# Splitting expert weights one ahead, and a position table in two rounds of products

## The chip, the cores and the metric

The kernel runs on one core of a Trainium2 chip. The metric is the device time of one execution in microseconds (us). The core has five engines that run at the same time and wait for each other through semaphores: TensorE (PE) multiplies, VectorE (DVE) and ScalarE (ACT) do elementwise work and empty PSUM, GpSimd (POOL) here mostly issues indirect transfers, and SyncE (SP) issues most other transfers. Each engine works through its own instructions strictly in order.

## The reference

A decoder layer on 1024 tokens of width 1024: attention and a convolution (they end before the part that is changed), then a mixture of experts, then a last norm. What matters here:

```python
grp = argmax(g_logits)                      # one of 4 groups, then 2 of its 8 experts per token
eid = grp * 8 + top_idx                     # 32 experts, 2048 assignments
buf_tok, buf_w = tokens and weights of each expert, sorted by expert
def expert_block(xblk, e):
    return (silu(xblk @ w_gate[e]) * (xblk @ w_up[e])) @ w_down[e]     # 1024 -> 512 -> 1024, float32
out[tok] += y * w                           # sum of the two experts of each token
```

Each expert has three weights of 2 MB, all 32 experts are read, and which tokens go to which expert is known only after routing.

## The kernel before, in words

The mixture runs over 32 *positions* e = 0 to 31. Positions 0 to 3 serve experts 0 to 3 with up to 128 tokens each. Positions 4 to 31 serve the other experts in an order that the kernel works out on the chip from the token counts: the 13 positions in `PK` take experts with at most 64 tokens ("packed"), position `XP` = 17 takes the fullest one and a second helping of 64 tokens (index `E`), the rest have 128.

**Weights.** The 96 weights are read in the order of the list `uses`: (e,0) gate, (e,1) up, (e-1,2) down, and so on. `load_to` issues them on SP's queue into a ring of eight slots of 2 MB, each as two halves of 1 MB (line 595), so a load waits until the weight eight places before it has left its slot. For positions from 4 on the load needs the expert's number, which SP reads from the tile `pos` (line 925).

**Unpacked positions** multiply in a split form: ACT rounds a quarter of a weight (128x1024) to `ehi` (line 102), DVE computes the rest `elo` (line 105), and PE makes three products of 128x512 for each of two k (lines 1024 to 1026 for gate and up, 1099 to 1101 for down). There are `NP` = 4 pairs of buffers, that is, one whole weight. `products` takes a quarter, multiplies, and calls `split_next`, which splits the next quarter in the list `pieces`. That list holds only the 57 unpacked weights. Once a weight's quarters are split, its slot is free.

**Packed positions** use the weight as it was loaded (lines 1014 and 1082), with two halves of the array side by side. So between two unpacked weights in `pieces` there can be up to three packed ones in `uses`: after (5,1) come (4,2), (6,0), (6,1), all packed, and then (5,2). Before the change the quarters of (5,2) are split while (5,1) is multiplied.

**Order.** PE, DVE and ACT run in the order in which the loop at the end of the function is written (a manual schedule). Each piece of a gate or up weight is followed by one `tick`, which takes one step from the list `todo`: a position's turn of its hidden rows, the scaling of its output, or a step of `position_tables`.

**Position table.** `position_tables` is a generator. It counts tokens per expert, ranks the experts, writes `pos`, and reorders the tokens' table `tb` into `half_t` and `late_t`, which the gathers from position 4 on need. Eight of its steps are queued in e = 0, the rest in e = 1. Nine of its steps have products on PE (lines 1138, 1143, 1168 and 1169, 1178 twice, 1187 and 1189 four times), each into the same PSUM tile `py`, and each is read by DVE before the next may write it.

Of the kernel before, what the change touches and what calls it, by code (L numbers as in the profile page):

```python
# [9 lines left out]
F32 = mybir.dt.float32  # L10
# [3 lines left out]
OP = mybir.AluOpType  # L14
# [5 lines left out]
D = 1024  # L20
H = 8
E = 32
F = 512
CW = 31
P = 128
# [8 lines left out]
LO = 4  # L34
XP = 17
# [8 lines left out]
def trunk_kernel(ctx, tc, x, c, w_mod, b_mod, g_norm1, w_in, conv_w, conv_b, conv_ln_g, conv_ln_b,  # L44
                 w_out, g_norm2, w_rg, b_rg, w_re, b_re, w_gate, w_up, w_down, g_final,
                 alibi, cst, out):
    nc = tc.nc
    x = x[0]
# [21 lines left out]
    ident = consts.tile([P, P], F32, name="ident")  # L70
    nc.sync.dma_start(ident, cst[:, 0:P])
    ones = consts.tile([P, P], F32, name="ones")
# [863 lines left out]
        split(hi, lo, wt[u][:, 2 * j:2 * j + 2, :])  # L936
        parts[u, j] = hi, lo

    def split_next():
        if pieces:  # L940
            u, j = pieces.pop(0)
            load_to(u)
            split_w(u, j)
# [10 lines left out]
    def products(u, mm, last=None):  # L954
        for j in range(4):
            if u[0] > E:
                split_w(u, j)
            mm(j, *parts.pop((u, j)))
            if j == 3 and last:
                last()  # L960
            if u[0] < E:
                split_next()
            yield

    def run(g):
# [33 lines left out]
    def gate_up(e, i):  # L999


        u = e, i
        o = st["o", e, i] = psg.tile([P, F], F32, name=("pg", "pu")[i])
        if e in PK or e == E:
            w = wt[XP if e == E else e, i]
            x4 = st["x", e]
            if e == E:
                xs = x4.rearrange("p a (b t) -> p (a b) t", b=2)
                x = lambda k: xs[:, k, :]
            else:  # L1010
                x = lambda k: x4[:, k % 4, k // 4 * 64:k // 4 * 64 + 64]
            for k in range(8):
                for c in range(2):
                    nc.tensor.matmul(o[64 * c:64 * c + 64, 0:256], x(k), w[:, k, 256 * c:256 * c + 256],  # L1014
                                     start=(k == 0), stop=(k == 7), skip_group_check=True)
                if k % 2:
                    yield
        else:
            xh, xl = st["x", e]

            def mm(j, hi, lo):
                for kk in range(2):
                    k = 2 * j + kk
                    nc.tensor.matmul(o, xh[:, k, :], hi[:, kk, :], start=(k == 0), stop=False)  # L1024
                    nc.tensor.matmul(o, xh[:, k, :], lo[:, kk, :], start=False, stop=False)  # L1025
                    nc.tensor.matmul(o, xl[:, k, :], hi[:, kk, :], start=False, stop=(k == 7))  # L1026

            yield from products(u, mm, (lambda: hidden(e)) if i else None)
        if i == 0:
            hs = st["h", e] = moe.tile([P, F], F32, name="hs")  # L1030
            n = 256 if e in PK or e == E else F
            nc.scalar.activation(hs[:, 0:n], o[:, 0:n], AF.Silu)
        elif e in PK or e == E:
            hidden(e, 256)
# [39 lines left out]
    def down(e):  # L1074

        t = st.pop(("t", e))
        if e in PK or e == E:
            wd = wt[XP if e == E else e, 2].rearrange("p (k a) f -> p k (a f)", a=2)
            py = psg.tile([P, F], F32, name="pg") if e == E else psx.tile([P, D], F32, name="py")[:, 0:512]
            for k in range(4):  # L1080
                for g in range(2):
                    nc.tensor.matmul(py[64 * g:64 * g + 64, :], t(k), wd[:, k, 512 * g:512 * g + 512],
                                     start=(k == 0), stop=(k == 3), skip_group_check=True)
                yield
            o2 = [(slice(64 * g, 64 * g + 64), slice(0, 512), py[64 * g:64 * g + 64, :],
                   slice(512 * g, 512 * g + 512)) for g in range(2)]
            if e == E:
                si, ws = [t[:, E - LO:E - LO + 1] for t in half_t]
            else:
                si, ws = slots(e)  # L1090
            w, n = 512, 2
        else:
            hh, hl = t
            py = psx.tile([P, D], F32, name="py")
            halves = [py[:, 0:512], py[:, 512:1024]]

            def mm(k, hi, lo):
                for half, o in enumerate(halves):
                    nc.tensor.matmul(o, hh[:, k, :], hi[:, half, :], start=(k == 0), stop=False)  # L1099
                    nc.tensor.matmul(o, hh[:, k, :], lo[:, half, :], start=False, stop=False)  # L1100
                    nc.tensor.matmul(o, hl[:, k, :], hi[:, half, :], start=False, stop=(k == 3))  # L1101

            yield from products((e, 2), mm)
            o2 = [(slice(0, P), slice(512 * i, 512 * i + 512), o, slice(512 * i, 512 * i + 512))
                  for i, o in enumerate(halves)]
            si, ws = slots(e)
            w, n = D, 1
        ys = moe.tile([P, D], F32, name="ys")[:, 0:w]

        def scale(i):  # L1110
            ps, sl, o, gl = o2[i]
            v.scalar_tensor_tensor(ys[ps, sl], o, ws[ps], gt2b[ps, gl], op0=OP.mult, op1=OP.mult)  # L1112
            if i:
                scatter(ys, si, n)

        todo.extend([lambda: scale(0), lambda: scale(1)])

    def pth(p, n):
        return psx.tile([P, D], F32, name="py")[0:p, 0:n]
# [12 lines left out]
    def position_tables():  # L1132
# [1 line left out]
        tmp = Scratch()  # L1134
        n = E - LO

        pb = pth(P, E)
        nc.tensor.matmul(pb, ones, Cc, start=True, stop=True)
        yield
        kb = tmp(P, E)  # L1140
        v.scalar_tensor_tensor(kb, pb, float(E), iota[:, 0:E], op0=OP.mult, op1=OP.add)
        pc = pth(E, 1)
        nc.tensor.matmul(pc, Cc, ones[:, 0:1], start=True, stop=True)
        yield
        cnt, kc, first, r = [tmp(E, 1) for i in range(4)]
        v.tensor_copy(cnt, pc)
        v.scalar_tensor_tensor(kc, cnt, float(E), tok1[0:E, 0:1], op0=OP.mult, op1=OP.add)
        v.tensor_scalar(first, tok1[0:E, 0:1], LO + 0.5, float(P), op0=OP.is_lt, op1=OP.mult)
        yield
# [1 line left out]
        v.tensor_scalar(m, kb[0:E, LO:], kc, None, op0=OP.is_lt)  # L1151
        v.tensor_reduce(r, m, axis=AX.X, op=OP.add)
        v.tensor_add(r, r, first)
        pi = tmp(E, n)
        v.tensor_scalar(pi, rankp[0:E, :], r, None, op0=OP.is_equal)
        yield

        v.tensor_mul(m, pi, capp[0:E, :])
        v.tensor_reduce(caps[:, 0:1], m, axis=AX.X, op=OP.add)
        v.tensor_add(caps[:, 0:1], caps[:, 0:1], first)  # L1160
        v.tensor_sub(cnt, cnt, caps[:, 0:1])
        v.tensor_scalar(cnt, cnt, float(P), None, op0=OP.add)
# [1 line left out]
        nb = tmp(E, 8)  # L1164
        v.tensor_tensor(nb, cnt.to_broadcast([E, 8]), lev[0:E, :], op=OP.is_gt)
        v.tensor_reduce(caps[:, 1:2], nb, axis=AX.X, op=OP.add)
        pp = pth(1, E + 1)
        nc.tensor.matmul(pp[:, LO:E], tok1[0:E, 0:1], pi, start=True, stop=True)
        nc.tensor.matmul(pp[:, E:E + 1], caps[:, 1:2], ones[0:E, 0:1], start=True, stop=True)
        yield  # L1170
        v.tensor_scalar(pos[:, LO:E], pp[:, LO:E], -1.0, None, op0=OP.add)
        v.tensor_copy(pos[:, E:E + 1], pp[:, E:E + 1])

        tT = moe.tile([P, D], F32, name="ys")[0:E, :].rearrange("e (q a s) -> e q a s", q=2, a=4)
        for q in range(2):
            pt = pth(E, 4 * P)
            for a in range(4):
                nc.tensor.matmul(pt[:, a * P:a * P + P], tb[:, a, q, :], ident, start=True, stop=True)
            yield
            v.tensor_copy(tT[:, q], pt.rearrange("e (a s) -> e a s", a=4))  # L1180

        def by_position(q, c0, c1, dst, halves=False):
            pt = pth(P, 4 * (c1 - c0))
            for a in range(4):
                sl = slice(a * (c1 - c0), (a + 1) * (c1 - c0))
                for h in range(2) if halves else ():
                    nc.tensor.matmul(pt[64 * h:64 * h + 64, sl], tT[:, q, a, 0:64], pi[:, c0:c1], start=True, stop=True)
                if not halves:
                    nc.tensor.matmul(pt[:, sl], tT[:, q, a, :], pi[:, c0:c1], start=True, stop=True)
            yield  # L1190
            t = tmp(P, 4 * (c1 - c0))
            v.tensor_copy(t, pt)
            tables(t.rearrange("p (a e) -> p a e", a=4), dst, moe, halves)

        yield from by_position(0, 0, n, [t[:, 0:n] for t in half_t], True)
        yield from by_position(0, 0, n, [t[:, 0:n] for t in late_t])
        x = XP - LO
        yield from by_position(1, x, x + 1, [t[:, n:n + 1] for t in late_t])
        yield from by_position(1, x, x + 1, [t[:, n:n + 1] for t in half_t], True)

    def overflow_tables():

# [73 lines left out]

    with tc.manual_schedule(engines={mybir.EngineType.PE, mybir.EngineType.DVE, mybir.EngineType.Activation}):
        for n in range(NP):
            split_next()
        for f in steps(0):  # L1280
            f()
        table = position_tables()
        for e in range(E):
            load_to((e, 0))
            if e < 2:
# [132 lines left out]
```

## Time and profile before

| | |
|---|---|
| median of 3 runs | 1235.61 us (1233.15 to 1236.14) |
| the profiled execution | 1232.49 us, of which the span from first to last instruction is 1230.7 us |
| busy over the span | PE 88%, DVE 64%, ACT 42%, POOL 18% |
| read from HBM, written | 275.75 MB, 26.23 MB |
| mean granted TensorE clock | 0.933 of full speed |

The mixture's first products start at 604.94 us and its last end before 1200 us; after it, the sum is read back, normed and written. Shares over the whole span mix the attention, the start of the mixture and its long even stretch, so they have to be read stretch by stretch. Times in the rows below are from the start of the span.

### The profile page before, as it was taken

Reading aid. Unit: us, or ns where it says so; the run is one execution under the profiler, and the core shown is the slowest. Engines: PE = TensorE matmul, PEld = TensorE weight load, DVE = VectorE, ACT = ScalarE, POOL = GpSimd, SP = SyncE. Lnnn points to the kernel's source line nnn. Section 1 sums busy time; section 2 is a strip of 40 time slices with the busy share of each in tenths; the row PEclk is TensorE's granted clock in tenths of the full one; section 3 lists DMA queues with packets and bytes.
Section 4 is the critical chain, followed back from the end, with each engine's and each line's share of the span. In section 5 each row is a group of like instructions: output and inputs, shape, how many; then the busy total and the mean of one; then the engine's idle time right before and its main releaser. Section 6 shows DMA issues by size and latency. Waiting matters only on the chain. (4 is left out here: it accounts for less than half of the span.)

```text
span 1230.7 us, 16064 instructions
## 1 busy us (share of the span) xinstructions
PE 1088.1 (88%) x5876; PEld 795.1 (65%) x5876; DVE 790.8 (64%) x1307; ACT 517.1 (42%) x795; POOL 223.2 (18%) x204
## 2 busy tenths in 40 slices
PE   4899999998999999999366999997979999799980
PEld 0667777786666667888344877775746677577750
DVE  1458999993664567676533976664645477566753
ACT  1431111114767653232222765553535455455622
POOL 2340000006121105001300222221211123112112
PEclk9899999998999999999666999998989999989995
DMA  9542534202001018538532999999999999999947
GB/s 366 185 154 92 216 127 147 103 12 74 20 17 36 1 59 304 214 131 306 198 122 76 309 376 406 409 407 388 390 383 353 398 392 402 380 399 392 371 117 283
DMA packets 60828, 292.65 MB, mean 238 GB/s; under 512 B 11861, under 2 KB 16213, under 8 KB 33092
## 3 DMA queue, kind: packets, MB, share of 16 engines
q1 hardware_dynamic: 48020, 253.16, 52.5%
q0 software_dynamic: 11296, 34.17, 9.8%
q10 hardware_dynamic: 1424, 4.20, 0.8%
q8 instruction: 48, 0.79, 0.3%
q14 instruction: 40, 0.33, 0.1%
HBM read 275.75 MB, written 26.23 MB: 245 GB/s over the span
## 5 line engine op out<-in xcount | busy, mean ns | idle before, releaser
L105 DVE TENSOR_TENSOR elo<-raw,ehi 128x1024 fp32r<-128x1024 f32 x228 | 273.3, 1223 | 113.9 <-ACT ehi L102 110.0
L102 ACT CAST ehi<-raw 128x1024 fp32r<-128x1024 f32 x228 | 237.9, 1049 | 159.6 <-PE pg L1026 55.5
L317 DVE SCALAR_TENSOR_TENSOR cv<-cv,cwT 128x1024 f32<-128x1024 f32 x120 | 154.1, 1284 | 3.6
L269 PE MATMUL pb<-hT,whi 128*128 128x512 f32 x256 | 100.8, 394 | 1.7 <-POOL hT L98 1.3
L268 PE MATMUL pb<-hT,whi 128*128 128x512 f32 x256 | 101.8, 399 | 0.0
L270 PE MATMUL pb<-hT,wlo 128*128 128x512 f32 x256 | 100.4, 393 | 0.6 <-DVE wlo L105 0.6
L1069 POOL DMA_INDIRECT x1d<-ys,ti x19 | 40.2, 2116 | 133.8 <-DVE ys L1112 127.0
L1024 PE MATMUL pg<-ehi,xh 128*128 128x512 f32 x152 | 64.0, 421 | 0.0
L1038 DVE TENSOR_TENSOR hs<-hs,pu 128x512 f32<-128x512 f32 (+1 forms) x33 | 18.9, 572 | 69.2 <-PE pu L1014 64.3
L1024 PE MATMUL pu<-ehi,xh 128*128 128x512 f32 x152 | 62.4, 410 | 0.0
L1099 PE MATMUL py<-ehi,hh 128*128 128x512 f32 x152 | 62.3, 410 | 0.0
L268 PEld LDWEIGHTS pb<-hT,whi 128*128 128x128 f32 x256 | 48.1, 188 | 21.8 <-ACT whi L102 9.2
L1025 PE MATMUL pu<-elo,xh 128*128 128x512 f32 x152 | 61.6, 405 | 0.0
L1026 PE MATMUL pu<-ehi,xl 128*128 128x512 f32 x152 | 61.5, 405 | 0.0
L1025 PE MATMUL pg<-elo,xh 128*128 128x512 f32 x152 | 61.4, 404 | 0.0
L1026 PE MATMUL pg<-ehi,xl 128*128 128x512 f32 x152 | 61.3, 403 | 0.0
L1100 PE MATMUL py<-elo,hh 128*128 128x512 f32 x152 | 59.6, 392 | 0.0
L1101 PE MATMUL py<-ehi,hl 128*128 128x512 f32 x152 | 59.5, 391 | 0.0
L269 PEld LDWEIGHTS pb<-hT,whi 128*128 128x128 f32 x256 | 48.1, 188 | 13.1 <-POOL hT L98 2.9
L1014 PE MATMUL pg<-raw,x 128*64 128x256 f32 x448 | 56.4, 408 | 0.0
L270 PEld LDWEIGHTS pb<-hT,wlo 128*128 128x128 f32 x256 | 48.1, 188 | 10.7 <-DVE wlo L105 1.0
L916 POOL DMA_INDIRECT xe<-h2d,ti x20 | 26.5, 1327 | 147.2 <-PE pt L994 121.2
(274 smaller groups left out, 2242.1 us busy)
## 6 DMA issues: line engine op xcount, KB each, us to landing
raw<-in_w_exp_gate_dram SPq DMA_DIRECT2D x64, 1024.0 KB, 19.5
raw<-in_w_exp_up_dram SPq DMA_DIRECT2D x64, 1024.0 KB, 23.2
raw<-in_w_exp_down_dram SPq DMA_DIRECT2D x64, 1024.0 KB, 21.3
wm<-in_w_mod_dram POOLq DMA_DIRECT2D x16, 1024.0 KB, 5.1
wm<-in_w_mod_dram SPq DMA_DIRECT2D x8, 1024.0 KB, 9.6
raw<-in_w_in_dram SPq DMA_DIRECT2D x3, 2048.0 KB, 9.7
xt<-in_x_dram SPq DMA_DIRECT2D x8, 512.0 KB
raw<-in_w_in_dram SPq DMA_DIRECT2D x4, 1024.0 KB, 11.9
```

What stands on the lines that cost most here:

```text
L102: nc.scalar.copy(hi, src)
L105: nc.vector.tensor_sub(lo, src, hi.bitcast(F32))
L268: nc.tensor.matmul(p[half], hi[:, k, :], hT[0][:, k, sl], start=(k == 0), stop=False)
L269: nc.tensor.matmul(p[half], hi[:, k, :], hT[1][:, k, sl], start=False, stop=False)
L270: nc.tensor.matmul(p[half], lo[:, k, :], hT[0][:, k, sl], start=False, stop=(k == 7))
L317: nc.vector.scalar_tensor_tensor(y, u[:, j:j + T], w, y, op0=OP.mult, op1=OP.add)
L1024: nc.tensor.matmul(o, xh[:, k, :], hi[:, kk, :], start=(k == 0), stop=False)
L1025: nc.tensor.matmul(o, xh[:, k, :], lo[:, kk, :], start=False, stop=False)
L1026: nc.tensor.matmul(o, xl[:, k, :], hi[:, kk, :], start=False, stop=(k == 7))
L1099: nc.tensor.matmul(o, hh[:, k, :], hi[:, half, :], start=(k == 0), stop=False)
L1100: nc.tensor.matmul(o, hh[:, k, :], lo[:, half, :], start=False, stop=False)
L1101: nc.tensor.matmul(o, hl[:, k, :], hi[:, half, :], start=False, stop=(k == 3))
```

## The change

It has two parts. (1) `split_next` now splits a quarter only if its weight is at most one place in `uses` after the weight being multiplied, and only if a pair of buffers is free; packed positions call it too, after every second k of gate and up and after every k of down. (2) `position_tables` has two rounds of products in place of nine. The first (counts, and the transposes of `tb`) is issued before position 0's own transposes, and ACT copies it out of PSUM. The second (the positions, and all four reorderings) is one run of products in e = 0 behind an empty step, and ACT copies it out; DVE's steps then read only SBUF. `pos` is written in the ninth step in place of the seventh.

```diff
+    at = {u: n for n, u in enumerate(uses)}
+    def split_next(now):
-        if pieces:
+        if pieces and len(parts) < NP and at[pieces[0][0]] <= now + 1:
             u, j = pieces.pop(0)
             load_to(u)
             split_w(u, j)
...
             if u[0] < E:
-                split_next()
+                split_next(at[u])
             yield
...
                 if k % 2:
+                    split_next(at[XP if e == E else e, i])
                     yield
...
+                split_next(at[XP if e == E else e, 2])
                 yield
...
-        pb = pth(P, E)
-        nc.tensor.matmul(pb, ones, Cc, start=True, stop=True)
+        pc = psx.tile([P, 4, P], F32, name="pth").rearrange("p a b -> p (a b)")
+        nc.tensor.matmul(pc[:, 0:E], ones, Cc, ...)
+        nc.tensor.matmul(pc[0:E, E:E + 1], Cc, ones[:, 0:1], ...)
+        pt = psx.tile([P, D], F32, name="py")[0:E, :]
+        for q in range(2):
+            for a in range(4):
+                nc.tensor.matmul(pt[:, (4 * q + a) * P:(4 * q + a + 1) * P], tb[:, a, q, :], ident, ...)
+        pb = tmp(P, E + 1)
+        nc.scalar.copy(pb[:, 0:E], pc[:, 0:E])
+        nc.scalar.copy(pb[0:E, E:E + 1], pc[0:E, E:E + 1])
+        tT = moe.tile([P, D], F32, name="ys")[0:E, :]
+        for q in range(2):
+            nc.scalar.copy(tT[:, 512 * q:512 * q + 512], pt[:, 512 * q:512 * q + 512])
         yield
...
+        yield
+        yield
+        pp = psx.tile([P, D], F32, name="py")
+        c = pp[:, 0:512]
+        nc.tensor.matmul(pp[0:1, 512 + LO:512 + E], tok1[0:E, 0:1], pi, ...)
+        nc.tensor.matmul(pp[0:1, 512 + E:512 + E + 1], caps[:, 1:2], ones[0:E, 0:1], ...)
+        jobs = ((0, 0, n, True), (1, x, x + 1, True), (0, 0, n, False), (1, x, x + 1, False))
+        for q, c0, c1, halves in jobs:
+            for a in range(4):
...
+        t = tmp(P, o)
+        nc.scalar.copy(t, c[:, 0:o])
+        pe = tmp(1, E + 1)
+        nc.scalar.copy(pe[:, LO:E + 1], pp[0:1, 512 + LO:512 + E + 1])
+        yield
+        yield
+        v.tensor_scalar(pos[:, LO:E], pe[:, LO:E], -1.0, None, op0=OP.add)
+        for (o, w), (q, c0, c1, halves) in zip(cols, jobs):
+            tables(t[:, o:o + 4 * w]..., d, moe, halves)
             yield
...
         for n in range(NP):
-            split_next()
+            split_next(0)
+        table = position_tables()
+        next(table)
         for f in steps(0):
             f()
-        table = position_tables()
```

## Rows read from the trace of the kernel before

**Rows 1.** Stretches of the span (start:end in us, length, busy time of each engine).

```profile
core 0: us, PE busy (x) PEld busy (x) DVE busy (x) ACT busy (x) POOL busy (x), PEclk, DMA share, GB/s
600.00:678.00 78.00, 49.68 (x186) 36.97 (x187) 27.12 (x58) 20.17 (x23) 2.03 (x3) 0.62 0.34 117
678.00:829.00 151.00, 151.00 (x838) 114.83 (x837) 114.50 (x122) 91.76 (x109) 31.87 (x19) 1.00 1.00 384
...
1076.00:1174.00 98.00, 94.46 (x492) 70.43 (x493) 71.47 (x76) 57.10 (x69) 18.17 (x10) 0.96 0.99 378
1174.00:1200.00 26.00, 21.51 (x128) 13.86 (x126) 11.56 (x14) 5.40 (x7) 4.52 (x3) 0.98 0.42 98
700.00:720.00 20.00, 20.00 (x95) 16.73 (x95) 19.51 (x20) 16.20 (x18) 6.95 (x3) 1.00 1.00 358
```

**Rows 2.** Timeline of SP's queue: weight loads (start us, us, instruction, count).

```profile
598.08 2.60 SPq L595 DMA_DIRECT2D raw<-in_w_exp_gate_dram  x2
...
650.65 13.23 SPq L595 DMA_DIRECT2D raw<-in_w_exp_gate_dram  x2
677.34 4.42 SPq L595 DMA_DIRECT2D raw<-in_w_exp_up_dram  x2
...
1161.20 2.81 SPq L595 DMA_DIRECT2D raw<-in_w_exp_down_dram  x2
```

**Rows 3.** Timeline of PE, positions 0 and 1 (brackets: idle before, releaser).

```profile
604.94 0.77 PE L1024 MATMUL pg<-ehi,xh 128*128 128x512 f32 x1
...
607.64 0.47 PE L1138 MATMUL py<-Cc,ones 128*128 128x32 f32 x2
...
629.98 1.91 PE L1178 MATMUL py<-ident,tb 128*32 128x128 f32 x8 [2.54 <-DVE pos L1172]
...
639.64 1.12 PE L994 MATMUL pt<-ident,xe 128*128 128x128 f32 x4
...
643.79 0.77 PE L1024 MATMUL pg<-ehi,xh 128*128 128x512 f32 x1
...
656.44 1.87 PE L1189 MATMUL py<-ys 32*128 32x28 f32 x8 [2.67 <-DVE ys L1192]
...
671.09 1.02 PE L1187 MATMUL py<-ys 32*64 32x1 f32 x16 [2.56 <-DVE ys L1192]
...
678.56 0.60 PE L994 MATMUL pt<-ident,xe 128*128 128x128 f32 x4
...
685.35 0.48 PE L1024 MATMUL pg<-ehi,xh 128*128 128x512 f32 x1
...
690.91 0.39 PE L1024 MATMUL pu<-ehi,xh 128*128 128x512 f32 x1
```

**Rows 4.** Timeline of ACT, one split in the same stretch.

```profile
653.81 1.04 ACT L102 CAST ehi<-raw 128x1024 fp32r<-128x1024 f32 x1 [4.75 <-PE pg L1026]
```

**Rows 5.** Timeline of DVE: the table's input, and what stands ahead of one round.

```profile
594.98 0.42 DVE L883 COPY tb<-ptab 128x256 f32<-128x256 f32 x1
...
654.89 1.23 DVE L105 TENSOR_TENSOR elo<-raw,ehi 128x1024 fp32r<-128x1024 f32 x1 [3.68 <-ACT ehi L102]
656.03 0.27 DVE L1192 COPY ys<-py 128x112 f32<-128x112 f32 x1
```

**Rows 6.** Waits from 600 to 1200 us (total us, times, longest).

```profile
ACT ehi L102 <- DMA raw<-in_w_exp_down_dram: 37.4, 10, 11.0
```

**Rows 7.** Timeline of ACT, the last long stall.

```profile
1074.47 1.99 ACT L102 CAST ehi<-raw 128x1024 fp32r<-128x1024 f32 x2 [2.01 <-DMA raw<-in_w_exp_down_dram]
```

**Rows 8.** Timeline of PE around it.

```profile
1065.78 3.65 PE L1082 MATMUL py<-raw,h 128*64 128x512 f32 x16
...
1077.43 1.13 PE L1063 MATMUL pth<-ident,hs 128*128 128x128 f32 x4 [8.00 <-DVE hs L1038]
...
1084.27 3.62 PE L1014 MATMUL pu<-raw,x 128*64 128x256 f32 x32
...
1088.29 0.49 PE L1099 MATMUL py<-ehi,hh 128*128 128x512 f32 x1
```

More of the change, by code (lines that the diff above doesn't have):

```diff
@@ L937, in split_w @@
         parts[u, j] = hi, lo
-    def split_next():
-        if pieces:
+    at = {u: n for n, u in enumerate(uses)}
+    def split_next(now):
+        if pieces and len(parts) < NP and at[pieces[0][0]] <= now + 1:
             u, j = pieces.pop(0)
@@ L1135, in position_tables @@
         n = E - LO
-        pb = pth(P, E)
-        nc.tensor.matmul(pb, ones, Cc, start=True, stop=True)
+        pc = psx.tile([P, 4, P], F32, name="pth").rearrange("p a b -> p (a b)")
+        nc.tensor.matmul(pc[:, 0:E], ones, Cc, start=True, stop=True, skip_group_check=True)
+        nc.tensor.matmul(pc[0:E, E:E + 1], Cc, ones[:, 0:1], start=True, stop=True, skip_group_check=True)
+        pt = psx.tile([P, D], F32, name="py")[0:E, :]
+        for q in range(2):
+            for a in range(4):
+                nc.tensor.matmul(pt[:, (4 * q + a) * P:(4 * q + a + 1) * P], tb[:, a, q, :], ident, start=True, stop=True,
+                                 skip_group_check=True)
+        pb = tmp(P, E + 1)
[4 more added lines that the diff above has]
+            nc.scalar.copy(tT[:, 512 * q:512 * q + 512], pt[:, 512 * q:512 * q + 512])
+        tT = tT.rearrange("e (q a s) -> e q a s", q=2, a=4)
         yield
         kb = tmp(P, E)
[L1141 to L1146, printed above, removed]
+        v.scalar_tensor_tensor(kb, pb[:, 0:E], float(E), iota[:, 0:E], op0=OP.mult, op1=OP.add)
+        cnt = pb[0:E, E:E + 1]
+        kc, first, r = [tmp(E, 1) for i in range(3)]
         v.scalar_tensor_tensor(kc, cnt, float(E), tok1[0:E, 0:1], op0=OP.mult, op1=OP.add)
@@ L1153, in position_tables @@
         v.tensor_add(r, r, first)
+        yield
         pi = tmp(E, n)
         v.tensor_scalar(pi, rankp[0:E, :], r, None, op0=OP.is_equal)
-        yield
         v.tensor_mul(m, pi, capp[0:E, :])
         v.tensor_reduce(caps[:, 0:1], m, axis=AX.X, op=OP.add)
+        yield
         v.tensor_add(caps[:, 0:1], caps[:, 0:1], first)
@@ L1166, in position_tables @@
         v.tensor_reduce(caps[:, 1:2], nb, axis=AX.X, op=OP.add)
-        pp = pth(1, E + 1)
-        nc.tensor.matmul(pp[:, LO:E], tok1[0:E, 0:1], pi, start=True, stop=True)
-        nc.tensor.matmul(pp[:, E:E + 1], caps[:, 1:2], ones[0:E, 0:1], start=True, stop=True)
         yield
-        v.tensor_scalar(pos[:, LO:E], pp[:, LO:E], -1.0, None, op0=OP.add)
-        v.tensor_copy(pos[:, E:E + 1], pp[:, E:E + 1])
-        tT = moe.tile([P, D], F32, name="ys")[0:E, :].rearrange("e (q a s) -> e q a s", q=2, a=4)
@@ L1175, in position_tables @@
-        for q in range(2):
-            pt = pth(E, 4 * P)
-            for a in range(4):
-                nc.tensor.matmul(pt[:, a * P:a * P + P], tb[:, a, q, :], ident, start=True, stop=True)
-            yield
[L1180 to L1199, printed above, removed]
+        yield
+        pp = psx.tile([P, D], F32, name="py")
+        c = pp[:, 0:512]
+        nc.tensor.matmul(pp[0:1, 512 + LO:512 + E], tok1[0:E, 0:1], pi, start=True, stop=True, skip_group_check=True)
@@ new lines, in position_tables @@
+        nc.tensor.matmul(pp[0:1, 512 + E:512 + E + 1], caps[:, 1:2], ones[0:E, 0:1], start=True, stop=True,
+                         skip_group_check=True)
+        x = XP - LO
+        jobs = ((0, 0, n, True), (1, x, x + 1, True), (0, 0, n, False), (1, x, x + 1, False))
+        o = 0
+        cols = []
+        for q, c0, c1, halves in jobs:
+            w = c1 - c0
+            for a in range(4):
+                sl = slice(o + a * w, o + a * w + w)
+                for h in range(2) if halves else ():
+                    nc.tensor.matmul(c[64 * h:64 * h + 64, sl], tT[:, q, a, 0:64], pi[:, c0:c1], start=True, stop=True,
+                                     skip_group_check=True)
+                if not halves:
+                    nc.tensor.matmul(c[:, sl], tT[:, q, a, :], pi[:, c0:c1], start=True, stop=True, skip_group_check=True)
+            cols.append((o, w))
+            o += 4 * w
@@ new lines, in position_tables @@
+        t = tmp(P, o)
[3 more added lines that the diff above has]
+        yield
+        yield
+        v.tensor_scalar(pos[:, LO:E], pe[:, LO:E], -1.0, None, op0=OP.add)
+        v.tensor_copy(pos[:, E:E + 1], pe[:, E:E + 1])
+        for (o, w), (q, c0, c1, halves) in zip(cols, jobs):
+            d = [t_[:, n:n + 1] if q else t_[:, 0:n] for t_ in (half_t if halves else late_t)]
+            tables(t[:, o:o + 4 * w].rearrange("p (a e) -> p a e", a=4), d, moe, halves)
+            yield
```

## The prediction

> **What bounds the kernel now.** I read the span stretch by stretch first, because the whole-span shares mix phases. The mixture has three phases. From 600 to 678 us nothing is busy: PE 49.68 of 78 us at a granted clock of 0.62, the DMA engines 0.34, 117 GB/s. From 678 to 1174 us the DMA engines are busy all the time at 378 to 384 GB/s, while PE is busy 151 of 151 us at first and 94.46 of 98 at the end. From 1174 us the transfers fall off (0.42) and PE still works off 21.51 us [rows 1]. So the long stretch is a stream of weights with PE close behind it, and it is early or late as a whole: its start is set by the first phase, its tail by how far PE lags when the last weight lands.
>
> Why is the first phase slow? SP's queue shows the loads waiting for slots: the ninth weight (gate of position 3) is issued at 598.08, the twelfth (gate of position 4) only at 650.65, the thirteenth at 677.34 [rows 2]. A slot opens when its weight has been split, and a quarter is split when PE has used up the one before. So the stream waits for PE. PE in turn shows a repeating pattern: from the round of table products at 656.44 to the one at 671.09 are two rounds, 7.3 us each, with six matmuls of real work between rounds and an idle of 2.56 to 2.67 us before each that DVE ends [rows 3]. The chain is serial: six matmuls end, ACT splits (1.04 us), DVE splits (1.23), DVE reads the table's last product (0.27), and only then may PE issue the next table product, with the matmuls of the expert queued behind it [rows 3 to 5]. The six matmuls, which need none of this, wait in line. That PE runs at the low one of its two clocks there (0.62 on average, against 1.00 from 678 us on) is a consequence of these gaps [rows 1].
>
> From four products of experts' weights, (0,0), (0,1), (1,0), (1,1), the first phase makes 604.94 to 678.56 = 73.6 us [rows 3].
>
> **The table, rebuilt step by step.** With the rounds gone, the same stretch costs:
> - Four weights at the pace of an undisturbed one, 685.35 to 690.91 = 5.56 us: 22.2 us [rows 3].
> - The clock is low at the start. Before, the first six matmuls took 604.94 to 607.64 = 2.70 us, where a quarter at the pace above is 1.39. I take two quarters at that price, +2.6; bounds: one quarter (+1.3), all sixteen (+21) if the clock never rises. The last is not likely, since PE then has no gaps [rows 3].
> - Transposes of position 1 and the turn of position 0, 639.64 to 643.79: 4.2 us, unchanged (3 if the clock is high) [rows 3].
> - Second round of products: two sets like 656.44 (1.87) and two like 671.09 (1.02), 5.8 us at the low clock, half at the high one, and at worst one wait as before (2.67). I take 5; bounds 3 and 8.4 [rows 3].
> - DVE's small steps. Each is at most as long as the copy at 656.03 (0.27), some four to five per step, so up to 1.1 us; with a split (1.23) they pass the 1.39 us that a quarter takes PE, in about four steps of position 1. Overrun up to 4.4, I take 2; none if they fit [rows 3, 5].
>
> Sum 22.2 + 2.6 + 4.2 + 5 + 2 = 36.0 against 73.6: the stretch ends **37.6 us** earlier (bounds 31.8, from 22.2 + 2.6 + 4.2 + 8.4 + 4.4 = 41.8, and 44, from 22.2 + 1.3 + 3 + 3 = 29.5).
>
> What moves is covered. The first round can start when `tb` is copied (594.98 + 0.42 = 595.4); its eight transposes are two groups like 629.98, 1.91 each [rows 3, 5]. The counts add less than 1, so it ends near 600.2 and leaves the time until the products at 604.94, in which PE has only position 0's transposes. If that cover were gone it would cost 4.8 us once. The four copies that ACT takes over are single instructions; priced like a quarter's split (1.04) they are 4.2 us and end near 604 at worst, so they may hold the first x split by a microsecond. `pos` moves two steps later. On SP only the twelfth load and what is queued behind it wait for it; the slot for that load opens when (1,1) has been split, later than the ninth step, so the move costs nothing. It would cost only if `pos` came after that.
>
> **Does the stream follow?** In the new first phase four loads have to be issued in some 40 us in place of 79: that is 2 MB in about 10 us, well under 384 GB/s [rows 1, 2]. From the thirteenth load on, the slots open at the same pace as before, so I shift the whole stream by the 37.6 us. A small debt is possible: before, the twelfth weight had landed when the thirteenth was issued, now it is still on its way (2 MB at 384 GB/s, 5.4 us); as in 700 to 720 us the stream runs at 358 GB/s for want of free slots, it can catch up there [rows 1]. I count 0, bound -4.
>
> **The split bound.** ACT waited ten times, 37.4 us in all, for a down weight still in flight [rows 6]. That is a weight up to four places ahead in `uses`: nine of the 57 unpacked weights have three packed ones before them. The wait stands in ACT's and DVE's queues ahead of work that is due. At 1074.47 ACT begins the second pair of splits of such a weight, whose half has just landed, and the hidden rows (line 1038) of the present position are queued behind them on DVE; PE idles 8.00 us at 1077.43, although the two packed weights it should multiply next were loaded earlier [rows 7, 8]. With the bound the split comes behind them. PE is free at 1065.78 + 3.65 = 1069.4; turn 1.13, gate and up 3.62 each, transposes 0.60 (as at 678.56): 1078.4 instead of 1088.29 for the first product of the late weight, whose second half landed by 1074.47, so it is not late [rows 3, 7, 8]. Gain 9.9 us of PE's lag.
>
> For the earlier stalls of this kind I count nothing: the DMA engines are saturated through them, and PE meets the stream again. The last one counts, because the stretch behind it (94.46 of 98 us busy) has no slack in which the lag was made up, and PE still has 21.51 us of work when the transfers fall off [rows 1]. I take **9** for it; bounds 0 (the stream holds PE back instead) and 10. Calling `split_next` in packed positions adds no instruction, it moves 16 weights' splits into the packed weight just before. That weight takes PE 3.62 us; four splits of 1.23 on DVE take 4.9, behind one of 1.04 on ACT, but PE needs one quarter per 1.39 us, so only the first is waited for, if any [rows 3 to 5, 8].
>
> Sum 37.6 + 9 = 46.6 from the profiled 1232.49: 1185.9. The median of the runs is 3.1 above the profiled execution, so I forecast 1189.
>
> **Rivals.**
> - *Only the table pays.* The stalls on weights in flight reappear as PE's own waits for the same weights and the tail stays: 1235.6 - 37.6 = 1198. For it: the DMA engines are never idle after 678 us, so PE can't win over the whole stretch [rows 1].
> - *More than forecast.* Clock up at once, no overrun, 10 in the tail: 1235.6 - 54 = 1182 and, if slots also open sooner where PE lagged, some 4 less, 1178.
> - *The stream can't keep its rate.* If it ran at 358 GB/s, as in 700 to 720 us, throughout, the 496 us from 678 to 1174 would be 532, +36, and 1225 would result. Against it: that row is short of slots, and the three long rows show 378 to 384 [rows 1]. The Trainium skill (DMA: Bandwidth & Descriptors, Where 436 GB/s comes from) has the HBM side bind at about 358 GB/s for loads into SBUF; by that rule the stream's length would come out as in this rival. The trace's 384 over 151 us is above it, so I give it little.
> - *Late splits (slower).* Sixteen unpacked weights come straight after a packed one. If their splits start only when PE stands at the weight, each costs 1.04 + 1.23 = 2.3 us, 36 us in all [rows 4, 5]; from 2.9 us each, with no stream to hide it, the gain of 46.6 is eaten, and at 4 us the time is 1253. For it: a packed weight is shorter than four splits. Against it: ACT and DVE have little else to do there.
> - *No change.* The first phase is bound by something else, the gathers or the loads of the first eight weights. Against it: the idle of PE there is ended by DVE each time [rows 3].
>
> **How the numbers follow.** Forecast 1189 (its own range 1181 to 1195): 0.58. Only the table: 0.18. More: 0.12. Rate lost or a first phase that stays slow, 1204 to 1225: 0.07. No change 0.02, late splits to the point of a loss 0.03. The low end takes in the "more" case with a microsecond of margin, 1177; the high end takes the table alone at its bound, 1235.6 - 31.8 = 1204. Range 1177 to 1204 leaves out the last three cases and some edges, under 2 in 10. About 0.3%, 3.7 us, is what a measurement can tell from no change. Faster 0.95, same 0.02, slower 0.03.
>
> **What would show it.** In the changed profile: no idle of PE on DVE between quarters of position 0, one at most before the second round; (1,1) ends near 641; the thirteenth load is issued near 640 and the DMA share is 1.00 from about 650; ACT's waits for down weights fall from 37.4 us to a few, and PE's 8 us stalls on line 1038 go; the last load is issued near 1124 and PE's tail after it is shorter by some 9 us. Wrong if the thirteenth load comes after 650, if the rate of the stream is under 375 GB/s, or if PE waits for splits after packed weights.

## The result, and the profile after

The changed kernel takes 1195.88 us (median of 4 runs, 1194.77 to 1199.56) against 1235.18 before (median of 4): a ratio of 0.9689, 95% interval [0.9664, 0.9714]. The forecast was 1189, range 1177 to 1204, and faster. The profiled execution went from 1232.49 to 1195.03 us, its span from 1230.7 to 1193.2, so 37.5 us are to be found in the trace.

Stretches of the changed kernel's span, in the columns of [rows 1]:

```profile
600.00:642.00 42.00, 35.04 (x167) 28.85 (x168) 23.25 (x48) 20.97 (x26) 2.42 (x3) 0.80 0.56 192
643.00:795.00 152.00, 152.00 (x839) 115.36 (x838) 115.42 (x123) 91.15 (x109) 35.13 (x20) 1.00 1.01 392
795.00:1140.00 345.00, 325.16 (x1787) 230.24 (x1785) 216.02 (x230) 170.36 (x207) 71.24 (x40) 0.99 1.00 382
1140.00:1166.00 26.00, 13.97 (x78) 7.93 (x74) 7.82 (x10) 2.48 (x5) 5.41 (x3) 0.92 0.44 97
```

The first phase ends at 642 instead of 678 us. From there the DMA engines are busy all the time again, at 382 to 392 GB/s, and the stretch is as long as before. SP's queue says the same; compare [rows 2], where the thirteenth weight went at 677.34 and the last at 1161.20:

```profile
598.46 2.60 SPq L595 DMA_DIRECT2D raw<-in_w_exp_gate_dram  x2
...
637.95 2.85 SPq L595 DMA_DIRECT2D raw<-in_w_exp_gate_dram  x2
643.48 3.21 SPq L595 DMA_DIRECT2D raw<-in_w_exp_up_dram  x2
...
1125.73 2.83 SPq L595 DMA_DIRECT2D raw<-in_w_exp_down_dram  x2
```

The thirteenth load is 33.9 us earlier, the last 35.5. Between them lie 483.9 us before and 482.3 after: the stream is shifted, not shortened.

PE in the first phase, which answers to [rows 3] (lines have moved: 1028 to 1030 are the products of 1024 to 1026, 997 the transposes of 994, 1148 the transposes of `tb`, 1202 and 1205 the reorderings):

```profile
595.84 3.40 PE L1148 MATMUL py<-ident,tb 128*32 128x128 f32 x16 [0.60 <-DVE tb L883]
601.95 0.92 PE L997 MATMUL pt<-ident,xe 128*128 128x128 f32 x4 [2.71 <-DMA xe<-h2d,ti]
...
605.09 0.78 PE L1028 MATMUL pg<-ehi,xh 128*128 128x512 f32 x1
...
616.72 0.21 PE L1189 MATMUL py<-ys,cs 32*1 32x28 f32 x2
618.20 0.18 PE L1190 MATMUL py<-ones,caps 32*1 32x1 f32 x2 [1.27 <-DVE caps L1183]
618.32 1.09 PE L1202 MATMUL py<-ys 32*64 32x28 f32 x32
619.34 3.56 PE L1205 MATMUL py<-ys 32*128 32x28 f32 x16
622.83 0.80 PE L1028 MATMUL pu<-ehi,xh 128*128 128x512 f32 x1
...
625.56 0.91 PE L997 MATMUL pt<-ident,xe 128*128 128x128 f32 x4
...
629.80 0.78 PE L1028 MATMUL pg<-ehi,xh 128*128 128x512 f32 x1
...
642.30 0.61 PE L997 MATMUL pt<-ident,xe 128*128 128x128 f32 x4
```

The first round is done before the gather has landed (601.95). After it there is one wait on DVE for the table, 1.27 us, where the kernel before had nine, of 0.49 to 4.04 us and 23.9 us in all. (1,1) ends at 642.30, where it ended at 678.56 [rows 3].

The stalls on a down weight in flight have not gone, they are spread. These are waits of the changed kernel between 640 and 1165 us (total us, times, longest; ACT's for weights in flight, and PE's first three); before, ACT had 37.4, 10, 11.0 for down weights [rows 6]:

```profile
ACT ehi L102 <- DMA raw<-in_w_exp_down_dram: 36.7, 13, 6.5
...
ACT ehi L102 <- DMA raw<-in_w_exp_up_dram: 8.3, 7, 2.5
...
ACT ehi L102 <- DMA raw<-in_w_exp_gate_dram: 3.3, 6, 0.8
...
PE py L1104 <- ACT ehi L102: 6.7, 4, 2.8
PE py L1105 <- DVE elo L105: 4.4, 7, 0.8
PE pu L1017 <- DMA raw<-in_w_exp_up_dram: 4.2, 5, 1.5
```

PE no longer stands 8 us at a turn [rows 8]; it waits a few us at a time for weights that have just landed. That is the rival's picture, "PE's own waits for the same weights". All the same PE idles less: in the stretch of 345 us that answers to 795 to 1140, it was busy for 316.77 us before and for 325.16 after.

```profile
829.00:1174.00 345.00, 316.77 (x1744) 227.49 (x1743) 216.60 (x228) 172.18 (x207) 66.93 (x40) 0.96 1.00 384
```

### The profile page after: what moved, and what is told of

Read it like the earlier page. It is cut to its first block, busy times and chain, and to the rows that moved or that the text cites. A ratio compares the mean times of both kernels' runs of the same rounds, so it can differ in the third digit from the quotient of the medians.

```text
span 1193.2 us, 16040 instructions
## 1 busy us (share of the span) xinstructions
PE 1079.5 (90%) x5876; PEld 788.5 (66%) x5876; DVE 784.2 (66%) x1300; ACT 514.3 (43%) x801; POOL 232.0 (19%) x204
## 5 line engine op out<-in xcount | busy, mean ns | idle before, releaser
L102 ACT CAST ehi<-raw 128x1024 fp32r<-128x1024 f32 x228 | 234.1, 1049 | 101.5 <-DMA raw<-in_w_exp_down_dram 36.7
L1073 POOL DMA_INDIRECT x1d<-ys,ti x19 | 44.9, 2361 | 129.2 <-DVE ys L1117 114.3
L1028 PE MATMUL pu<-ehi,xh 128*128 128x512 f32 x152 | 59.9, 394 | 0.0
L1017 PE MATMUL pu<-raw,x 128*64 128x256 f32 x448 | 51.6, 381 | 4.2 <-DMA raw<-in_w_exp_up_dram 4.2
L422 ACT ACTIVATE ns<-ns,st 128x128 f32<-128x128 f32 (+7 forms) x64 | 49.2, 772 | 9.2 <-DVE st L418 8.6
```

Source lines behind the costliest of these rows:

```text
L102: nc.scalar.copy(hi, src)
```

## The experiments

Two theories. **S**: the stream of weights sets the time from the thirteenth load on; the table moved its start, and the split bound can only shorten what PE has left after the last loads, some 3 us. **R**: the split bound is worth the 9 us that were predicted, and the table's part lost as much on the way.

One table serves all runs. Each entry is the start (us) of an instruction in that run's own trace: position 0's first transposes, the transposes behind (1,1), the thirteenth and the last weight's load, PE's last group (down of position 31), the first read-back of the sum. The first column moves by 5 us from run to run with what comes before the mixture, so the text compares differences between columns. Those of the first phase have a spread of their own: in the seven runs whose first phase is the changed kernel's, x(0) to (1,1) is 40.1 to 40.4 us in four and 38.5 in three (less stream with the old split, tail order, scale first), so there a difference under 2 us tells nothing.

| run | x(0) | (1,1) done | 13th load | last load | last group | read-back |
|---|---|---|---|---|---|---|
| before | 601.65 | 678.56 | 677.34 | 1161.20 | 1192.91 | 1205.40 |
| changed | 601.95 | 642.30 | 643.48 | 1125.73 | 1153.85 | 1167.82 |
| changed again | 602.43 | 642.82 | 644.18 | 1125.58 | 1153.69 | 1167.26 |
| table only | 598.81 | 638.95 | 639.96 | 1121.84 | 1153.22 | 1165.60 |
| bound only | 603.13 | 680.09 | 678.87 | 1163.18 | 1194.35 | 1206.69 |
| round twice | 598.93 | 644.01 | 645.40 | 1126.54 | 1154.67 | 1168.54 |
| less stream | 604.22 | 644.34 | 645.35 | 1099.65 | 1129.22 | 1141.55 |
| less stream, old split | 603.28 | 641.81 | 643.23 | 1094.34 | 1130.65 | 1143.73 |
| 64-column products | 603.48 | 643.17 | 644.20 | 1125.71 | 1155.31 | 1167.91 |
| first round late | 603.14 | 644.08 | 645.15 | 1128.77 | 1158.22 | 1171.67 |
| tail order | 603.66 | 642.17 | 643.57 | 1125.11 | 1155.49 | 1168.53 |
| scale first | 601.58 | 640.07 | 641.47 | 1123.08 | 1148.73 | 1162.31 |
| 64-column and scale first | 602.33 | 641.99 | 643.00 | 1124.41 | 1149.77 | 1162.08 |
| the same, at every packed position | 604.04 | 642.29 | 643.67 | 1125.73 | 1151.29 | 1164.49 |

**Each part alone.** "Table only" is the changed kernel with the split rule of before, that is, also without the calls in packed positions (the cut below). "Bound only" is the kernel before with the new split rule, and the table in nine rounds.

```diff
-        if pieces and len(parts) < NP and at[pieces[0][0]] <= now + 1:
+        if pieces:
...
-                    split_next(at[XP if e == E else e, i])
...
-                split_next(at[XP if e == E else e, 2])
```

> The table in two rounds, the split rule of before (a quarter is split as soon as a buffer is free, packed positions split nothing). Theory S (the stream of weights sets the length from the thirteenth load on; the split bound only shortens PE's tail by what was measured between the last load and PE's last group, some 3 us): 1196 to 1200 us. Rival R (the split bound is worth the 9 us that were predicted, and the table's part lost as much on the way): 1204 to 1206 us.

> The split bound alone, the table as before in nine rounds. Theory S: 1232 to 1235 us, since the stream still starts at 677 us. Rival R: 1226 us. A third reading (each part pays only with the other): 1235 or more.

The table alone takes 1195.10 us, ratio 0.9678 [0.966, 0.9695]: all of the gain. The bound alone takes 1231.93, 0.9974 [0.9956, 0.9992], some 3 us. R's 1204 and 1226 are both missed; S's ranges are met within 1 us. In the traces: from (1,1) to PE's last group are 514.4 us before and 514.3 with the table alone, the same work moved as one block; with both parts it is 511.6 and 510.9. With the bound alone it is 514.3, so its one profile does not show the 3 us that its runs have. The trace says why: in that execution (1234.10 us, where the median of its 12 runs is 1231.93) the granted clock was 0.65 over the products of (30,2), 1179.4 to 1189.1 us, and they took 9.7 us. In the changed kernel it was 1.00, and they took 6.9 (1141.7 to 1148.6). One product of each, from the timelines of PE of bound only and of the changed kernel:

```profile
1181.67 0.63 PE L1103 MATMUL py<-ehi,hh 128*128 128x512 f32 x1
...
1144.21 0.40 PE L1106 MATMUL py<-ehi,hl 128*128 128x512 f32 x1
```

Without these 2.8 us, bound only would have some 511.5 us, as with both parts; that is an estimate from the two stretches.

With the table alone, PE still has the stalls of before (waits of PE, 600 to 1200 us), and yet the last load is issued 481.9 us after the thirteenth, against 482.3 without them:

```profile
PE pth L1066 <- DVE hs L1041: 22.5, 4, 8.2
```

**A known delay in the first phase.** The reordering products of the second round are issued twice.

```diff
-            for a in range(4):
+            for a in (0, 1, 2, 3, 0, 1, 2, 3):
```

> The changed kernel with the 24 reordering products of the second round issued twice (same results written twice), so 4.5 us more PE work at the place of the table, nothing else. Theory S with a start that shifts the whole stream one to one: 1200 to 1201 us, (1,1) ends 4.5 us later, the last load is issued 4 to 5 us later. Rival (the stream has slack behind its start, and the 36 us of the first phase were passed on only in part): 1196 to 1198 us.

Measured 1199.43 us, ratio 0.9721 [0.9697, 0.9745]. From x(0) to (1,1) are 45.1 us where the changed kernel has 40.3 and 40.4, and from the thirteenth to the last load 481.1: the 4.7 us go through to the last load. From x(0) to the read-back are 569.6 us where the changed kernel has 565.9 and 564.8, so 3.7 to 4.8 of them reach the end: the first phase passes on what it loses, one to one within that spread. The times alone (1195.67 to 1202.59 in four runs) would not exclude the rival's 1196 to 1198; the traces do.

**A shorter stream.** The second half of the down weight of the 13 packed positions is not loaded (its products use what the slot held), PE's work is unchanged.

```diff
-            wt[p, i] = eload(wsrc(p, i, expert.get(p), p in PK))
+            wt[p, i] = eload(wsrc(p, i, expert.get(p), p in PK)[:1 if i == 2 and p in PK else 2])
```

> The changed kernel with the second half (1 MB) of the down weight of the 13 packed positions not loaded; their products take what the slot held. 13.6 MB less, 35 us of stream at 385 GB/s, with PE's work unchanged. Theory S: the end moves by as much as PE can follow, that is by PE's idle time between 795 and 1157 us, some 20 to 27 us: 1169 to 1178 us. Rival (PE's own chain of splits and products sets the length behind 643 us): 1190 us or more.

1166.41 us, ratio 0.9441 [0.9423, 0.9459], 29 us less, a little more than expected. The waits for landings are nearly gone (ACT's between 640 and 1130 us, which answer to the 36.7, 8.3 and 3.3 above):

```profile
ACT ehi L102 <- DMA raw<-in_w_exp_gate_dram: 2.9, 2, 1.8
ACT ehi L102 <- DMA raw<-in_w_exp_up_dram: 1.4, 2, 0.8
ACT ehi L102 <- DMA raw<-in_w_exp_down_dram: 1.1, 3, 0.5
```

and PE is busy nearly without a gap from 795 to 1095 us, where in the changed kernel it had 325.16 of 345 from 795 to 1140 (a stretch of the same run, in the columns of [rows 1]):

```profile
795.00:1095.00 300.00, 298.83 (x1691) 215.44 (x1690) 204.22 (x217) 159.32 (x196) 66.47 (x39) 1.00 1.00 385
```

So in the changed kernel the stream bounds the long stretch, and PE follows some 30 us behind it in work. Does the bound pay once the stream is out of the way? The same cut with the split rule of before:

> Half of the packed positions' down weights not loaded, as in the run with the shorter stream, but with the split rule of before. Theory S (ahead or behind, the bound decides nothing: with a full stream the landing sets the time, with a short one no split waits for a landing): 1165 to 1168 us, as with the bound (1166.4). Rival (with the stream out of the way the bound is worth PE's stalls): 1172 us or more.

1171.55 us, ratio 0.9508 [0.9465, 0.9552]. This lies between S's 1165 to 1168 and the rival's 1172, and next to the rival: S as stated fails, the bound decides something, 5 us by the medians, 3.9 by the traces ((1,1) to the last group 488.8 against 484.9). Where landings do not set the time, splits in their turn keep PE busier; where they do, it shows only in the tail.

**Where the tail's gain went.** With both parts the last group comes 28.1 us after the last load (28.1 to 29.6 in the runs that have both parts and the tail as it was, the shorter stream among them; 31.4 with the table alone), so PE won 1.8 to 3.3 us. The runs with some 29.5 (less stream, 64-column products, first round late) have a clock of 0.79 over the products of (30,2), those with 28.1 have 1.00. But from that group to the read-back it is 14.0 and 13.6 us where the table alone has 12.4. The tail of the changed kernel by the timelines of ACT, DVE, POOL and PE:

```profile
1136.86 1.99 ACT L102 CAST ehi<-raw 128x1024 fp32r<-128x1024 f32 x2 [5.07 <-DMA raw<-in_w_exp_down_dram]
...
1132.66 1.22 DVE L105 TENSOR_TENSOR elo<-raw,ehi 128x1024 fp32r<-128x1024 f32 x1
1137.94 1.23 DVE L105 TENSOR_TENSOR elo<-raw,ehi 128x1024 fp32r<-128x1024 f32 x1 [4.06 <-ACT ehi L102]
1139.08 0.74 DVE L1117 SCALAR_TENSOR_TENSOR ys<-py,ws,gt2b 128x512 f32<-128x512 f32 x1
...
1141.90 2.28 POOL L1073 DMA_INDIRECT x1d<-ys,ti  x1 [13.59 <-DVE ys L1117]
1152.36 1.55 POOL L1073 DMA_INDIRECT x1d<-ys,ti  x1 [8.18 <-DMA x1d<-ys,ti]
1160.28 1.57 POOL L1073 DMA_INDIRECT x1d<-ys,tih  x1 [6.37 <-issue]
...
1141.77 0.47 PE L1104 MATMUL py<-ehi,hh 128*128 128x512 f32 x1 [1.54 <-DVE ys L1117]
...
1143.41 0.50 PE L1106 MATMUL py<-ehi,hl 128*128 128x512 f32 x1 [0.94 <-DVE hl L105]
```

ACT waits 5.07 us for half of (30,2). The bound has put these splits into position 31's gate products, and the leftover steps (scaling of position 29's output, line 1117, and the split of position 30's hidden rows) stand behind them on DVE and ACT. So the scatter of position 29 leaves at 1141.90 although its products ended near 1136; the scatter of position 30 then waits 8.18 us for it to land. This is a new wait in the place of the old one. PE is held up by the same steps: 1.54 us by the scaling that frees `py`, 0.94 by the split of the hidden rows. To test it, the leftover steps are issued first:

```diff
             load_to((e, 0))
+            if e == E - 1:
+                flush()
```

> The changed kernel, but at position 31 the steps left over (scaling of position 29's output, splitting of position 30's hidden rows) are issued before the gate products, not between them, so that DVE does them before it waits for the splits of (30,2). Theory: the bound put those splits ahead of the scaling, and the scatter of position 29 left 7 us late; it now leaves some 5 us earlier (16.2 us after the last load was issued in the changed kernel), and the end comes 1 to 2 us earlier, 1193 to 1195 us. Rival (the end hangs on PE behind the landing of (30,2) alone): the scatter is earlier, the time stays at 1195 to 1196 us.

1192.43 us, ratio 0.9649 [0.9625, 0.9674]; the changed kernel run again has 1194.68, 0.9677 [0.965, 0.9705], so the times alone do not tell them apart. The trace does:

```profile
1133.86 1.41 DVE L1117 SCALAR_TENSOR_TENSOR ys<-py,ws,gt2b 128x512 f32<-128x512 f32 x2 [2.36 <-PE py L1106]
...
1135.55 1.55 POOL L1073 DMA_INDIRECT x1d<-ys,ti  x1 [9.61 <-DVE ys L1117]
1146.33 1.55 POOL L1073 DMA_INDIRECT x1d<-ys,ti  x1 [9.23 <-DMA x1d<-ys,ti]
1154.40 1.57 POOL L1073 DMA_INDIRECT x1d<-ys,tih  x1 [6.53 <-DVEq L1345]
```

The scatter of position 29 leaves 12.5 us after the last load, not 16.2, and the read-back comes 39.2 us after it, not 42.1 and 41.7: 2.5 to 2.9 us. Nearly all of this is PE's: both of its waits are gone, and its last group comes 25.7 us after the last load, not 28.1. The scatters had held up less: in the changed kernel the last one leaves 6.4 us after PE's last group, here 5.7, as with the table alone. From there to the read-back it is 6.6 to 7.9 us in all runs, and 7.9 in this one.

Of the changed kernel itself, run beside it:

> The changed kernel itself, beside the three above, so that they are compared on one chip: 1195 to 1197 us by either theory.

**Three that did not pay by themselves.** (a) The 128-column reorderings as two of 64 columns:

```diff
-                if not halves:
-                    nc.tensor.matmul(c[:, sl], tT[:, q, a, :], pi[:, c0:c1], ...)
+                for h in () if halves else range(2):
+                    nc.tensor.matmul(c[64 * h:64 * h + 64, sl], tT[:, q, a, 64 * h:64 * h + 64], pi[:, c0:c1], ...)
```

> The changed kernel, but the eight 128-column reordering products of the second round (3.56 us at line 1205) are written as two 64-column ones each, as the other eight pairs of the round (1.09 us at line 1202). If the first phase passes to the end one to one (theory S), the round gets 2.5 us shorter, perhaps 2 to 4 more where the clock then stays up, and the time is 2.5 to 6 us below the changed kernel: 1190 to 1193 us. Rival (the phase is bound by the splits behind the round): no change, 1196 us.

1194.23 us, 0.9666 [0.9641, 0.9691]: not told apart from the changed kernel. The group went from 3.56 to 1.80 us, but x(0) to (1,1) only from 40.3 to 39.7, which is inside the spread of that stretch; behind the group the clock was low in this execution too (below).

```profile
620.81 1.80 PE L1205 MATMUL py<-ys 32*64 32x28 f32 x32
```

(b) `next(table)` in front of position 0 left out, so that the first round runs in position 0's first step:

> The changed kernel with the first round not in front of position 0 but in its first step, all later steps one later. The prediction covered the round by the wait for the gather and priced it at 4.8 us if that cover is gone. Theory: (1,1) ends 3 to 6 us later than in the changed kernel and the time is 3 to 6 us longer, 1199 to 1202 us. Rival (the place makes no difference, the number of rounds alone counts): 1196 us.

1196.46 us, 0.9698 [0.9678, 0.9717], not told apart either; x(0) to (1,1) is 40.9 us, 0.5 to 2.4 more than in the seven runs above. The rival was right. The transposes of `tb` take 2.05 us there, at a granted clock of 0.91 (609.6 to 611.7 us), where in front of position 0 they take 3.40 at 0.56 (595.8 to 599.3 us of the changed kernel):

```profile
609.66 2.05 PE L1148 MATMUL py<-ident,tb 128*32 128x128 f32 x16
```

(c) (30,2) read and used before position 31's weights, with the leftover steps ahead of it:

> The changed kernel with the last down weight of an unpacked position, (30,2), read and used before the three packed weights of position 31 and not between them. Theory S with a tail that starts when that weight lands: it lands one weight (5.4 us) earlier, 18 us of PE work behind it then run while the last two weights land, the end is 2 to 4 us earlier than the changed kernel, 1192 to 1194 us. Rival (the tail is bound by the last landing, or PE waits for the hidden rows of position 30): 1196 us or more.

1196.51 us, 0.9694 [0.9675, 0.9714]: no gain. The rival's time was right, by another wait than its own: PE now stands before (30,2) for the scaling of position 29 that frees `py`, and the last group comes 30.4 us after the last load instead of 28.1.

```profile
1139.48 0.47 PE L1104 MATMUL py<-ehi,hh 128*128 128x512 f32 x1 [3.33 <-DVE ys L1117]
```

**Together.** The 64-column products and the leftover steps first at position 31, then the same at every packed position:

> Both small edits together: 64-column products in the second round and the left-over steps first at position 31. If both hold, 1191 to 1194 us, below the changed kernel by 0.1 to 0.3%; if the clock of the first phase takes back the one and the landing of (30,2) the other, 1195 us.

> As the run with both small edits, but the left-over steps go before the gate products at every packed position, not at position 31 alone. Theory (in the long stretch the landing of the weights sets the time, and only the tail keeps what DVE gains): no further change, 1187 to 1191 us, ratio 0.960 to 0.965. Rival (the splits in front of the scaling cost PE at every packed position): 5 to 10 us less, 1180 to 1185 us.

1189.11 us, ratio 0.9622 [0.9594, 0.9651], and 1189.97, 0.963 [0.9608, 0.9653]. The first beats both kernels, the changed one by 5.6 to 6.8 us (its interval ends where that of the changed kernel run again begins); the second adds nothing to it, as S has it for the long stretch.

## Why the prediction was right, step by step

- **What bounds the kernel: right.** The first phase was bound by the rounds of the table, and the stream shifts as a block: 514.4 and 514.3 us from (1,1) to PE's last group with the old and the new table, and a known delay of 4.7 us went through.
- **The table's 37.6 us: right, 36.3.** From the first products to the end of (1,1) are 37.2 us against 36.0 built. By its terms: the start's low clock cost 1.9 where 2.6 was taken (42 matmuls in 605.09 to 616.72 = 11.6 us, where at 0.23 us each they are 9.7); transposes and turn 625.56 to 629.80, 4.2 as taken; the second round 616.72 to 622.83, 6.1 where 5 was taken; DVE's overrun, taken as 2, does not show (the second half of (1,0) and (1,1) run at 0.23 us a matmul). Missing was that the clock falls behind the round: the last quarter of (0,1), 622.83 to 625.56, and the first of (1,0) take 2.7 us each again, 2.7 us above the pace for both. That the sum comes so near is in part luck: the overrun that did not come and the clock that was not foreseen nearly cancel.
- **The cover of the first round: right that it is hidden, wrong in its price.** Without the cover it costs 0.5 to 2.4 us by the trace and nothing that the times tell, not 4.8: inside the running products it meets the higher clock. That it stands in front is worth nothing that could be measured.
- **`pos` two steps later: wrong, it costs the twelfth load 1.1 us.** The argument was that its slot opens only when (1,1) has been split, later than the ninth step. But a weight is loaded as two halves, and its slot opens half by half. In the changed kernel the first half of (1,1) is split by 636.79, `pos` is written from 636.70 on and read by SP at 636.9, and the load goes at 637.95, 1.25 us after that writing began (1.25 or 1.26 us in every run with the new table). Before, the load went 0.02 us after the split (first line, of the kernel before; 650.65 [rows 2]):

```profile
649.41 1.22 DVE L105 TENSOR_TENSOR elo<-raw,ehi 128x1024 fp32r<-128x1024 f32 x1
...
635.57 1.22 DVE L105 TENSOR_TENSOR elo<-raw,ehi 128x1024 fp32r<-128x1024 f32 x1
636.70 0.16 DVE L1214 TENSOR_SCALAR pos<-ys 1x28 int32<-1x28 f32 x1
```

No run here shows what the 1.1 us are worth; the thirteenth load goes as its own slot opens.

- **The stream follows: right.** The debt (0 taken, bound -4) was 2.4 us at the thirteenth load, and 0.8 at the last. The rate rival is out: 392 GB/s over 152 us. The row that it rests on, 700 to 720 us, was read as short of slots; its DMA share is 1.00 [rows 1], so that this made its 358 GB/s is not shown. The rule named there, of the Trainium skill (DMA: Bandwidth & Descriptors, Where 436 GB/s comes from), that the HBM side binds at about 358 GB/s, does not hold for this core alone; the Trainium skill's page HBM Reference (Specifications) says that a core streaming alone gets well above its share, and these runs agree, with the 392 GB/s.
- **The split bound: the stall that it takes away is real, its price is wrong.** 9 us were taken at the end; with the table in place the runs show no difference (0.9689 and 0.9677 with it, 0.9678 without). The step that failed is that the last stretch had "no slack in which the lag was made up" and that PE would keep its lead to the end. PE did get ahead, by some 6 us and not 9: between the last load and the last group it has 24.16 us of work in the changed kernel (1125.7 to 1153.8 us) and 30.37 with the table alone (1121.8 to 1153.2), at a clock of 1.00 in both. But it idles for 3.9 us there instead of 1.0, for the landing of (30,2) and the steps behind its splits, and of its lead 3.3 us are left at the last group. To the read-back 1.7 to 2.1 are left (41.7 and 42.1 us after the last load, 43.8 with the table alone). The prediction named "the stream holds PE back instead" as the bound of 0, and the rival "only the table pays" with 1198: that is what came, 1196.
- **Its own signs.** As said: (1,1) near 641 (642.30), one wait before the second round, the last load near 1124 (1125.73), the 8 us stalls gone. Not as said: ACT's waits for down weights were to fall to a few us and are 36.7; PE's tail was to be shorter by some 9 us and is shorter by 3.6 (28.1 for 31.7). Of the three signs of being wrong one came: PE waits for splits in front of down weights, 6.7 us for ACT's and 4.4 for DVE's.

The forecast of 1189 was 7 us low for the split bound: of the 46.6 us built, the table gave 36.3 of its 37.6 and the bound 1 to 2 of its 9 by the traces, nothing by the runs. That the time lies inside the range is owed to the rival that set its upper part, not to the sum. The medians fell by 39.3 us, 1.8 more than the profiled executions; the one profiled before was 2.7 below its median.

## What to carry to other kernels

Where a long stretch is a saturated stream, ask first when it starts: what delays the first slots delays the end by as much, and every other stall in the stretch is worth only what is left of it after the last landing. A chain of small steps that go back and forth between PE and DVE costs by its number of crossings, with real work queued behind each; gathered into few rounds that a third engine copies out, it no longer holds up that work (fewer rounds and the third engine were not tried apart). When work that may wait for a transfer is moved, look at what now stands behind it in the same engine's queue: here the splits that freed the turn held up the scaling, PE behind it, and the scatters.

## What was not expected of the hardware

TensorE's granted clock has two levels here, 1.00 (2.4 GHz) and 0.50 (1.2 GHz); a mean in between is a mix of them. It fell inside the second round although PE was busy for most of it. Stretches of the changed kernel, in the columns of [rows 1]:

```profile
605.00:609.00 4.00, 4.00 (x12) 3.22 (x11) 0.69 (x1) 1.55 (x2) 0.99 (x1) 0.50 0.56 205
609.00:616.70 7.70, 7.70 (x34) 6.03 (x32) 6.28 (x17) 6.11 (x8) 0.00 (x0) 0.99 0.43 137
616.70:622.80 6.10, 4.83 (x53) 4.63 (x52) 3.68 (x5) 1.83 (x2) 0.00 (x0) 0.72 0.89 289
622.80:633.00 10.20, 7.91 (x27) 6.30 (x28) 3.21 (x4) 2.79 (x6) 0.99 (x1) 0.67 0.41 147
633.00:642.00 9.00, 9.00 (x41) 7.46 (x40) 8.00 (x20) 7.78 (x9) 0.00 (x0) 1.00 0.39 132
```

In the round PE issued 53 small matmuls, 4.83 us of 6.10 busy, with one wait of 1.27 us; the granted clock went from 0.99 to 0.72 and was 0.67 over the next 10 us. Inside the round it was still 1.00 over the 64-column group (618.2 to 619.3 us) and 0.51 over the 128-column group behind it (619.3 to 622.8). Whether the wait or the small products brought it down, no run separates. How soon it came back differs between executions of the same code: of the 54 matmuls from there to the end of (1,1), 12 to 14 ran at the low level in four of the seven runs named above and 6 in three, which is their spread of 1.6 us in that stretch. With the shorter group (64 columns) the clock was 0.50 from 622.5 to 634 us; for the same reason one execution does not show that the edit did it.

The products of 32 rows into 128 columns took 3.56 us for 16 records. The same work written into 64 columns, at the same place and the same low clock (0.52), took 1.80 us for 32; the group of that form in front of it, at 1.00, took 1.09.
